# A fused three-mixer decoder layer on one core: the attention values of two pairs of heads in one group, even heads first

## The chip, the core and the metric

The kernel runs on one core of a Trainium2 chip. The metric is the device time of one execution in microseconds (us); three runs of the kernel before have a median of 263.72 us.

## What is computed

One decoder layer on a sequence of 256 positions with 1024 channels. A projection of the input feeds three mixers (a gated spatial MLP, a convolution module, attention with 8 heads of 64), their gates and the gates of a merge; each mixer's result is projected to 1024 channels, the three are merged, projected once more, added to the input and normalised. The part that the change touches is the last product of the attention and its gate. With a sequence of 256 and a block of 256 the attention is plain causal attention:

```
p   = softmax(q k^T / 8 - slope * distance)      # per head, causal
att = p @ v                                      # per head: 256 x 64
y_c = att * silu(c_g)
```

## The kernel before, in words

Everything is in float32. The large matrix products split each operand into a high part (hi, the cast to the TensorE's rounded float32 format, made by ScalarE at L92) and a low part (lo, the difference, made by VectorE at L93) and add three products, or two with a double-width moving operand. `gemm_tok` (L206, matmuls at L96 to L98) makes tiles with positions on the partitions, `gemm_ch` (L222, matmuls at L229 and L230) tiles with channels on the partitions. PLAN (L43) lists the blocks of the projection in the order in which they are computed: among them the query, key and value blocks, then the gate blocks `c_g` and `b_g`, then the first merge block `m0a`. Weights are loaded and split two to three half-blocks ahead (L596).

Between the blocks stand the small steps of the mixers. Which step is emitted behind which block is written out by hand in AFTER (L580): one list of steps for the middle of a block and one for its end. The framework then orders each engine's instructions itself: a step that was emitted later can be placed earlier, into a time at which the scheduler expects the engine to wait, and a step whose operands the scheduler expects late is placed later.

The steps of the attention, for each of the four pairs j of heads (2j is the even head, 2j + 1 the odd one; r is 0 or 1):

- `scores(j)` (L377) and `softmax(j)` (L391) leave the normalised probabilities in `lg[j]`: for each head 384 columns, 128 for the first 128 queries and 256 for the other 128 queries.
- `turn(j)` (L410) transposes the three 128 x 128 blocks of each head on TensorE (L415) and ScalarE copies them into a tile `turned` (L417). There are four buffers of `turned`, so two pairs of heads at a time.
- `values(j)` (L419) multiplies with the values (L426). Per head two matmuls: keys 0 to 127 for all 256 queries (256 columns, starts the sum) and keys 128 to 255 for the queries 128 to 255 (128 columns, adds to it). The stationary operand is 64 columns wide, the head's part of `v`; the output of an even head stands on partitions 0 to 63 of the accumulator `att`, that of an odd head on partitions 64 to 127, so that an even head uses the left half of TensorE's columns and an odd head the right half. The order of the four matmuls of a pair is even 256, odd 256, even 128, odd 128. Two pairs share one accumulator `att[j // 2]`, one of the four `aux` buffers in PSUM; after the second pair VectorE multiplies with the gate (L434) and the result is split into `yh[2]` and `yl[2]` (L435).

AFTER emits `turn(0)` and `turn(1)` at the end of block `c_g`; `values(0)`, `values(1)`, `turn(2)` and `turn(3)` in this order at the end of `b_g`; `values(2)` and `values(3)` in the middle of `m0a`.

## Time and profile before

| | before |
|---|---|
| median of 3 runs | 263.72 us (263.62 to 264.7) |
| the profiled execution's own time | 263.93 us |
| its span, first to last instruction | 262.2 us |
| TensorE (PE) busy | 253.0 us, 96% of the span |
| VectorE (DVE) busy | 214.1 us, 82% |
| ScalarE (ACT) busy | 151.2 us, 58% |
| matmuls of line 426 | 32 records for 16 instructions |

The profile shows one execution. The time outside of the span is 263.93 - 262.2 = 1.7 us. PE is TensorE's matmuls and PEld its loads of stationary operands, which run beside them. A matmul with plain float32 operands and a 64-column output appears as two records, two passes over its columns. Matmuls are pipelined: the time between two starts tells what one costs, and the duration of a record is longer than that.

### The profile page before, as it was taken

The page shows a single profiled execution, that of the slowest core. Times are in us where ns is not written, and L with a number is a line of the kernel's source. Part 1 is how long each engine was busy: PE and PEld are TensorE (multiplying, and loading weights), DVE is VectorE, ACT ScalarE, POOL GpSimd, SP SyncE. Part 2 cuts the span into 40 slices and gives each one's busy share as a digit, 9 for nine tenths or more (in the row PEclk, how much of TensorE's full clock was granted, in tenths as well). Part 3 has the DMA queues.
Part 4 walks back from the last instruction along what each step waited for, and adds up shares of the span by engine and source line. Part 5 has one row for each costly group of instructions (what it writes and reads, how often), then busy time and mean ns, then how long its engine had stood idle before and what let it go on. Part 6 is the DMA issues. An engine that isn't in the chain of part 4 may idle for free.

```text
span 262.2 us, 3445 instructions
## 1 busy us (share of the span) xinstructions
PE 253.0 (96%) x1284; PEld 212.4 (81%) x1284; DVE 214.1 (82%) x324; ACT 151.2 (58%) x220; POOL 20.4 (8%) x29
## 2 busy tenths in 40 slices
PE   6999999999999999999999999999999999999990
PEld 4888888889888888888877888888888888888880
DVE  1899998798389999999998999994689564794644
ACT  4884887999994446376556342354433895191201
POOL 6003000000000000000000000005054000000202
PEclk9999999999999999999999999999999999999996
DMA  6999999534435445484444354465543592000112
GB/s 183 345 422 411 420 415 336 191 135 162 160 120 200 159 164 180 157 302 164 161 162 160 111 209 164 142 220 214 225 162 139 189 373 102 0 0 0 44 39 80
DMA packets 9952, 49.31 MB, mean 188 GB/s; under 512 B 1104, under 2 KB 2512, under 8 KB 5072
## 3 DMA queue, kind: packets, MB, share of 16 engines
q1 hardware_dynamic: 9360, 48.51, 50.0%
q10 hardware_dynamic: 576, 0.59, 0.8%
q8 instruction: 10, 0.16, 0.2%
q14 instruction: 6, 0.05, 0.0%
HBM read 48.04 MB, written 1.05 MB: 187 GB/s over the span
## 4 chain that ended last, share of the span: by engine, by line
PE 73%; issue 21%; POOL 2%; DMA 1%; ACT 0%; POOLq 0%; SPq 0%; DVE 0%
PE mm L229 17%; PE mm L96 14%; PE mm L97 14%; PE mm L98 14%; PE mm L230 9%; PE aux L426 1%; DMA raw<-in_wts_dram 1%; PE aux L415 1%; POOL br L198 1%; PE aux L385 1%; PE aux L383 1%; PE aux L253 1%; POOL res L539 0%; POOL vr L198 0%; PE aux L450 0%
## 5 line engine op out<-in xcount | busy, mean ns | idle before, releaser
L92 ACT CAST hi<-raw 128x2048 fp32r<-128x2048 f32 (+3 forms) x64 | 83.1, 1319 | 66.3 <-PE mm L98 33.8
L93 DVE TENSOR_TENSOR lo<-raw,hi 128x2048 fp32r<-128x2048 f32 (+3 forms) x64 | 98.6, 1553 | 21.4 <-ACT hi L92 21.1
L229 PE MATMUL mm<-xs,hi 128*128 128x512 f32 x192 | 68.3, 399 | 0.0
L96 PE MATMUL mm<-hi,xs 128*128 128x512 f32 (+1 forms) x162 | 62.7, 396 | 1.0 <-ACT hi L92 1.0
L97 PE MATMUL mm<-lo,xs 128*128 128x512 f32 (+1 forms) x162 | 63.5, 392 | 0.0
L98 PE MATMUL mm<-hi,xs 128*128 128x512 f32 (+1 forms) x162 | 63.3, 391 | 0.0
L230 PE MATMUL mm<-xs,lo 128*128 128x256 f32 x192 | 54.0, 281 | 0.0
L280 DVE SCALAR_TENSOR_TENSOR cv<-glu,ch,cv 128x256 f32<-128x256 f32 x120 | 50.2, 477 | 0.0
L229 PEld LDWEIGHTS mm<-xs,hi 128*128 128x128 f32 x192 | 36.1, 188 | 8.8 <-DVE cv L280 0.2
L96 PEld LDWEIGHTS mm<-hi,xs 128*128 128x128 f32 x162 | 30.8, 193 | 7.5 <-ACT hi L92 1.5
L97 PEld LDWEIGHTS mm<-lo,xs 128*128 128x128 f32 x162 | 31.0, 191 | 6.7 <-issue 0.6
L230 PEld LDWEIGHTS mm<-xs,lo 128*128 128x128 f32 x192 | 36.3, 189 | 0.1
L98 PEld LDWEIGHTS mm<-hi,xs 128*128 128x128 f32 x162 | 31.0, 191 | 6.2
L97 PE MATMUL mm<-lo,yh 128*128 128x512 f32 x48 | 18.9, 393 | 0.0
L98 PE MATMUL mm<-hi,yl 128*128 128x512 f32 x48 | 18.8, 391 | 0.0
L96 PE MATMUL mm<-hi,yh 128*128 128x512 f32 x48 | 18.7, 389 | 0.0
L96 PE MATMUL mm<-hi,mth 128*128 128x512 f32 (+1 forms) x40 | 14.0, 349 | 0.0
L97 PE MATMUL mm<-lo,mth 128*128 128x512 f32 (+1 forms) x40 | 13.9, 349 | 0.0
L98 PE MATMUL mm<-hi,mtl 128*128 128x512 f32 (+1 forms) x40 | 13.7, 347 | 0.0
L470 ACT ACTIVATE gate<-mm 128x512 f32<-128x512 f32 x12 | 6.9, 596 | 11.2 <-PE mm L98 10.9
L297 POOL TENSOR_TENSOR csa<-cv 128x512 f32<-128x512 f32 x1 | 1.3, 1287 | 149.3 <-DVE cv L280 149.3
L234 ACT COPY low<-mm 128x256 f32<-128x256 f32 x24 | 8.5, 364 | 4.1 <-PE mm L230 4.0
(112 smaller groups left out, 250.8 us busy)
## 6 DMA issues: line engine op xcount, KB each, us to landing
raw<-in_wts_dram SPq DMA_DIRECT2D x38, 1024.0 KB, 4.8
raw<-in_wts_dram SPq DMA_DIRECT2D x4, 512.0 KB, 7.4
raw<-in_wts_dram SPq DMA_DIRECT2D x7, 256.0 KB, 5.6
xres<-in_x_dram SPq DMA_DIRECT2D x2, 512.0 KB, 6.1
fvec<-in_rows_dram SPq DMA_DIRECT2D x2, 512.0 KB, 8.0
out_dram<-res SPq DMA_DIRECT2D x4, 208.0 KB, 2.0
xr<-in_xt_dram SPq DMA_DIRECT2D x2, 256.0 KB, 6.1
vec<-in_rows_dram SPq DMA_DIRECT2D x1, 512.0 KB, 10.2
```

Of the source, the lines that this page charges most:

```text
L92: nc.scalar.copy(hi, src)
L93: nc.vector.tensor_tensor(lo, src, hi.bitcast(F32), op=ALU.subtract)
L96: nc.tensor.matmul(o, s[0], m[0], start=start, stop=False)
L97: nc.tensor.matmul(o, s[0], m[1], start=False, stop=False)
L98: nc.tensor.matmul(o, s[1], m[0], start=False, stop=stop)
L198: nc.gpsimd.tensor_tensor(r, ve, nhalf[:, 0:n], op=ALU.pow)
L229: nc.tensor.matmul(pt, his[i][:, cols], xs[k // 2][:, k % 2], start=k == 0, stop=False)
L230: nc.tensor.matmul(pt[:, 0], los[i][:, cols], x_part(k, 0), start=False, stop=k == KD - 1)
L234: nc.scalar.copy(low, pt[:, 1])
L253: nc.tensor.matmul(pz[:, g], sg_raw[:, g], vn[:, t, P * g:P * (g + 1)], start=True, stop=True)
L280: nc.vector.scalar_tensor_tensor(cv[:, c], src, w, cv[:, c], op0=ALU.mult, op1=ALU.add)
L470: nc.scalar.activation(gates[n][:, t], pt, AF.Sigmoid)
```

## The change

`values` is called once for two pairs (h = 0, 1) in place of once for each pair. It emits both even heads first, each with its 256-column and its 128-column matmul, and then both odd heads. The gate's product and the split follow as before. The accumulator is a local tile. In AFTER the two calls of each place become one.

```diff
-    att, turned = {}, {}
+    turned = {}
...
-    def values(j):
-        if j % 2 == 0:
-            att[j // 2] = aux_ps.tile([P, 2, S], F32, name="aux")
-        for b, (keys, q) in enumerate(((0, slice(0, S)), (1, slice(P, S)))):
-            for r in range(2):
-                d = HD * (2 * j + r)
-                w = turned[j, r][:, 0:S] if b == 0 else turned[j, r][:, S:]
-                nc.tensor.matmul(att[j // 2][HD * r:HD * (r + 1), j % 2, q], v[:, keys, d:d + HD], w,
-                                 start=b == 0, stop=b == 1)
-        if j % 2 == 1:
-            h = j // 2
-            if h == 0:
-                new_y(2)
-            c = slice(2 * h, 2 * h + 2)
-            y = work.tile([P, 2, S], F32, name="y")
-            nc.vector.tensor_tensor(y, gate_c[:, c], att[h], op=ALU.mult)
-            split(yh[2][:, c], yl[2][:, c], y)
+    def values(h):
+
+        att = aux_ps.tile([P, 2, S], F32, name="aux")
+        for r in range(2):
+            for jj in range(2):
+                d = HD * (2 * (2 * h + jj) + r)
+                w = turned[2 * h + jj, r]
+                o = att[HD * r:HD * (r + 1), jj]
+                nc.tensor.matmul(o, v[:, 0, d:d + HD], w[:, 0:S], start=True, stop=False)
+                nc.tensor.matmul(o[:, P:], v[:, 1, d:d + HD], w[:, S:], start=False, stop=True)
+        if h == 0:
+            new_y(2)
+        c = slice(2 * h, 2 * h + 2)
+        y = work.tile([P, 2, S], F32, name="y")
+        nc.vector.tensor_tensor(y, gate_c[:, c], att, op=ALU.mult)
+        split(yh[2][:, c], yl[2][:, c], y)
...
-        "b_g": ([], [at(values, 0), at(values, 1), at(turn, 2), at(turn, 3)]),
-        "m0a": ([at(values, 2), at(values, 3)], []),
+        "b_g": ([], [at(values, 0), at(turn, 2), at(turn, 3)]),
+        "m0a": ([at(values, 1)], []),
```

## Rows read from the trace of the kernel before

**Rows 1.** The page: span, and each engine's busy time, share, instructions

```profile
span 262.2 us, 3445 instructions
PE 253.0 (96%) x1284; PEld 212.4 (81%) x1284; DVE 214.1 (82%) x324; ACT 151.2 (58%) x220; POOL 20.4 (8%) x29
```

**Rows 2.** Busy time by stretch (columns in the first row)

```profile
core 0: us, PE busy (x) PEld busy (x) DVE busy (x) ACT busy (x) POOL busy (x), PEclk, DMA share, GB/s
123.30:128.90 5.60, 5.60 (x42) 4.32 (x41) 5.60 (x11) 2.09 (x2) 0.00 (x0) 1.00 0.16 44
128.90:143.20 14.30, 14.30 (x73) 10.94 (x72) 13.38 (x24) 8.59 (x14) 0.00 (x0) 1.00 0.56 205
143.20:200.00 56.80, 56.80 (x254) 47.02 (x253) 48.43 (x66) 24.58 (x19) 10.23 (x5) 1.00 0.47 167
200.00:255.00 55.00, 55.00 (x275) 46.46 (x273) 35.74 (x46) 25.37 (x37) 1.73 (x3) 1.00 0.29 105
```

**Rows 3.** All matmuls of line 426

```profile
L426 PE MATMUL aux<-turned,v x32: 272/351/431, 123.4 to 142.6; 128*64 128x256 f32 x16, 128*64 128x128 f32 x16
```

**Rows 4.** PE's timeline around its first stretch of line 426 (start us, us, instruction)

```profile
122.82 0.28 PE L230 MATMUL mm<-xs,lo 128*128 128x256 f32 x1
122.94 0.39 PE L229 MATMUL mm<-xs,hi 128*128 128x512 f32 x1
123.17 0.28 PE L230 MATMUL mm<-xs,lo 128*128 128x256 f32 x1
123.38 0.87 PE L426 MATMUL aux<-turned,v 128*64 128x256 f32 x8
124.18 0.50 PE L229 MATMUL mm<-xs,hi 128*128 128x512 f32 x1
124.51 0.28 PE L230 MATMUL mm<-xs,lo 128*128 128x256 f32 x1
```

**Rows 5.** The same around the second stretch

```profile
126.98 0.28 PE L230 MATMUL mm<-xs,lo 128*128 128x256 f32 x1
127.19 0.87 PE L426 MATMUL aux<-turned,v 128*64 128x256 f32 x8
128.00 1.20 PE L415 MATMUL aux<-ident,lg 128*128 128x128 f32 x9
```

**Rows 6.** The same around the third stretch

```profile
134.74 0.49 PE L415 MATMUL aux<-ident,lg 128*128 128x128 f32 x3
135.16 1.29 PE L426 MATMUL aux<-turned,v 128*64 128x256 f32 x10
136.38 0.50 PE L97 MATMUL mm<-lo,xs 128*128 128x512 f32 x1
136.72 0.39 PE L98 MATMUL mm<-hi,xs 128*128 128x512 f32 x1
136.95 0.40 PE L96 MATMUL mm<-hi,xs 128*128 128x512 f32 x1
```

**Rows 7.** The same around the fourth stretch

```profile
141.73 0.39 PE L96 MATMUL mm<-hi,xs 128*128 128x512 f32 x1
142.05 0.86 PE L426 MATMUL aux<-turned,v 128*64 128x256 f32 x6
142.84 0.50 PE L97 MATMUL mm<-lo,xs 128*128 128x512 f32 x1
143.19 0.40 PE L98 MATMUL mm<-hi,xs 128*128 128x512 f32 x1
```

**Rows 8.** PE's timeline around eight transposes with 128-column outputs

```profile
118.23 0.40 PE L229 MATMUL mm<-xs,hi 128*128 128x512 f32 x1
118.47 1.04 PE L450 MATMUL aux<-ident,ya 128*128 128x128 f32 x8
119.26 0.36 PE L230 MATMUL mm<-xs,lo 128*128 128x256 f32 x1
119.46 0.40 PE L229 MATMUL mm<-xs,hi 128*128 128x512 f32 x1
```

**Rows 9.** Line 426 in flight at 123.70 and 123.85, then at 136.15 and 136.24 us

```profile
123.38 0.65 PE L426 MATMUL aux<-turned,v 128*64 128x256 f32 x4
123.64 0.50 PE L426 MATMUL aux<-turned,v 128*64 128x256 f32 x4
...
135.86 0.59 PE L426 MATMUL aux<-turned,v 128*64 128x256 f32 x2
136.07 0.38 PE L426 MATMUL aux<-turned,v 128*64 128x256 f32 x1
```

**Rows 10.** Line 426 by form to 142.10 and 142.25; in flight at 142.485, 142.49

```profile
L426 PE MATMUL aux<-turned,v x2: 323/376/430, 142.1 to 142.1; 128*64 128x256 f32 x1, 128*64 128x128 f32 x1
L426 PE MATMUL aux<-turned,v x3: 272/323/430, 142.1 to 142.2; 128*64 128x128 f32 x2, 128*64 128x256 f32 x1
142.22 0.48 PE L426 MATMUL aux<-turned,v 128*64 128x128 f32 x2
142.32 0.38 PE L426 MATMUL aux<-turned,v 128*64 128x256 f32 x1
```

**Rows 11.** ACT's copies of the turned heads, and DVE's two gate products (timelines)

```profile
116.48 0.52 ACT L417 COPY turned<-aux 128x384 f32<-128x384 f32 x1
129.77 1.24 ACT L417 COPY turned<-aux 128x384 f32<-128x384 f32 x3
137.04 0.47 ACT L417 COPY turned<-aux 128x384 f32<-128x384 f32 x1
...
129.19 0.67 DVE L434 TENSOR_TENSOR y<-gate_c,aux 128x512 f32<-128x512 f32 x1
142.95 0.69 DVE L434 TENSOR_TENSOR y<-gate_c,aux 128x512 f32<-128x512 f32 x1 [0.84 <-PE aux L426]
```

## The prediction

> **What bounds the kernel now.** I read the page's first lines first: TensorE is busy for 253.0 of 262.2 us [rows 1]. Then the busy time by stretch: from 123.3 us, where the changed matmuls begin, to 255 us, TensorE is busy in every microsecond at the full granted clock (1.00), while VectorE has room after 200 us and ScalarE throughout [rows 2]. So a microsecond that TensorE spends more or less between 123 and 143 us moves the end by about as much. Nothing in the change adds work to another engine or a DMA, so the question is what sixteen matmuls cost on TensorE and how they are placed.

> Next I looked at line 426 alone. Sixteen instructions are 32 records, 16 with 256 columns and 16 with 128 [rows 3], two passes each. They run in four stretches: two of 8 records, one of 10, one of 6 [rows 4 to 7].

> **What a stretch costs.** I measure from a neighbouring matmul before to one behind and take off what lies between these two normally.
> - First stretch: L230 at 123.17 to L230 at 124.51 is 1.34 us; the same step without it is 0.35 (122.82 to 123.17) [rows 4]. Cost 0.99 us.
> - Second: 126.98 to 128.00 is 1.02, normally 0.12 (123.17 against 122.94 is 0.23 for an L229, and 0.35 - 0.23 is left for an L230) [rows 4, 5]. Cost 0.90.
> - Third: L415 at 134.74 to L98 at 136.72 is 1.98; three transposes (0.11 each) and an L97 (0.23, as from L98 to L96) are 0.56 [rows 6]. Cost 1.42.
> - Fourth: L96 at 141.73 to L98 at 143.19 is 1.46, normally 0.46. Cost 1.00 [rows 6, 7].

> Together 4.3 us.

> The inside of a stretch tells more. In the first one, two 256-column records are in flight from 123.38 on, two more join from 123.64, and by 123.85 four are under way that began at 123.64 or later: records come in pairs, 0.22 us a pair [rows 9]. In the third, the last two records have no partner, and their starts are 0.21 us apart (135.86, 136.07) [rows 9]: they are the two passes of the even head of the fourth pair, whose odd head was turned only later. So a pair costs what a single pass costs: an even head on one half of the columns and an odd head on the other half run at the same time. A 256-column pass is 0.215 us, a 128-column pass half of that; two of each, a whole head, are **0.65 us**, and an odd head beside it is free. The first stretch has 0.65 us of this, which leaves 0.99 - 0.65 = **0.34 us** for going to 64-column outputs and back. The eight transposes with 128-column outputs show no such price: 118.23 to 119.46 is 1.23, less 0.35 is 0.88, that is 8 times 0.11 [rows 8].

> **What the change does to each stretch.** The number of matmuls, of columns, of weight loads and of products on VectorE is the same. What moves is the order. Before, neighbours are an even and an odd head. After, the first four matmuls are all even, the last four all odd.

> Where the stretches are cut is the scheduler's choice. The first stretch is placed in front of a matmul of `b_g`, ahead of where the source has it, and takes exactly four matmuls (256, 256, 128, 128 columns) before that matmul goes on; by then all four heads were turned (the fourth copy starts at 116.48 [rows 11]), so time, not data, ended it. In the new order the first four are 256, 128, 256, 128: the same columns after three and after four. I take the cut to stay there.
> - First stretch, four matmuls of even heads: nothing to run beside. 2 x 0.65 = 1.30 in place of 0.65. **+0.65 us.**
> - Second stretch, the four of the odd heads: the same, **+0.65 us**.
> - Third stretch: before, five matmuls, since the odd head of the fourth pair was not turned (its copy starts at 137.04 [rows 11]). The new order has six ahead of that head: both even heads and the odd head of the third pair. If the two halves of the columns take their work independently, the even half with 1.30 us sets the time, against 0.65 + 0.43 = 1.08 now: +0.22 us. If an odd head starts only when the even ones have all been started, it is 1.30 + 0.65 less one 128-column pass that can overlap, 1.84: +0.76 us.
> - Fourth stretch: before, the odd head's two matmuls with the even head's 128 columns beside; after, the odd head alone. 0.65 both times: **0**.

> The sum is **+1.5 us** with independent halves and **+2.1 us** with order kept. Which one? The fourth stretch shows that a half can run ahead: one 256-column and one 128-column record start together, and at 142.22 a second 128-column record has started while the second pass of the first 256-column matmul starts only at 142.32 [rows 10]. Both passes of the 128-column matmul thus overtook a pass that precedes them. That is a jump over one pass; the change asks for a jump over seven or eight. The nearest row shows independent halves, so I take +1.5 and keep +2.1 for the range. Below zero in the third stretch a reason excludes, as long as the cut stands: its even half grows.

> [...]

> The rest I cost at nothing. The gate product of the first two pairs starts at 129.19, and the second stretch ends about 128.0 now [rows 5, 11]; 1.3 us later it waits some 0.1 us, and behind it in VectorE's queue stands work for TensorE that is late by the same 1.3 us. The second product waits 0.84 us already [rows 11]; that wait moves along. The copies into `turned` at 129.77 need their buffers free, which is so when the second stretch is over, before and after; the transposes that feed them stand behind it on TensorE in both orders. If that cover were gone, each is bounded by a tenth or two. SP's queue and POOL's are not passed by anything that moves.

> The profiled execution took 263.93 us, 0.2 over the median of 263.72; added to the median, the forecast is **265.2 us**.

> **The rivals.**
> 1. *Order kept in the same cuts*: +2.1, 265.8 us. For it: the trace shows a jump over one pass only. Against: that jump [rows 10]. Chance 0.25. [...]
> 2. *Not slower: one stretch for each group of eight, halves independent.* The scheduler places a whole group where now two stretches are, and the odd half starts at once. Each group is then 1.30 + 0.34 = 1.64, two are 3.3 in place of 4.3: -1.0, **262.7 us**. It decides as soon as a visit holds both halves' four matmuls. For it: a visit's 0.34 us is real, and two would go. Against: the first cut was set by time, and the copy at 137.04 keeps the last head out of the third stretch. Chance 0.17.
> 3. *One stretch each, order kept*: 2 x 1.30 - 0.11 + 0.34 = 2.83 a group, +1.4, 265.1 us. Chance 0.06.
> 4. *It does not do what it says*: the scheduler mixes the halves again as it fills gaps, and the pairs remain: about 263.7 us. Against: in the third and fourth stretch it held back the even head's 128 columns, whose operand was there, behind the odd head's matmul, so it keeps the source's order within an accumulator. Chance 0.10.

> **How the numbers follow.** The forecast has the remaining 0.42. Half a percent, about what a measurement here can tell from no change, is 1.3 us: under 262.4 is faster, over 265.0 slower. The forecast lies just beyond, and 0.27 of its 0.42 is counted as slower; of rival 1 0.24, of rival 3 0.03: 0.54. Rival 2 lies inside, and 0.07 of it is counted as faster. The rest, 0.39, is no difference. The range is 262.9 to 266.1: it holds the forecast, rivals 1, 3 and 4 and the upper edge of rival 2.

> **What the profile would show.** Right: four stretches of line 426 with 8, 8, 12 and 4 records; in the first two all starts one behind the other, 0.21 and 0.11 us apart, and a cost of about 1.64 us each; then 1.64 and 1.0. The third tells forecast and rival 1 apart: 1.64 or 2.2. Wrong: 16 records in one stretch, or pairs of records from 123.4 us on.

## The result and the profile after

The changed kernel takes **265.49 us** (median of 6 runs, 264.96 to 266.18) against 263.92 us for the kernel before in the same runs: ratio 1.0052, 95% interval 1.0035 to 1.0069. The medians differ by 1.57 us. The ratio is an estimate of its own and not the quotient of the two medians (that is 1.0059); by it the changed kernel is slower by 1.4 us, between 0.9 and 1.8. The ratios further down are of the same kind, each against the kernel before in the same runs. The forecast was 265.2.

The profiled execution took 265.72 us. The first lines of its page:

```profile
span 264.0 us, 3446 instructions
PE 255.1 (97%) x1284; PEld 214.0 (81%) x1284; DVE 214.1 (81%) x324; ACT 151.3 (57%) x220; POOL 19.4 (7%) x29
```

Each engine has as many instructions as in [rows 1], TensorE is busy for 2 us more, and the span is 1.8 us longer. To see where, I take two matmuls that both kernels have: the first transposes of `turn_a`, ahead of all matmuls of `values`, and the first matmul of the first branch projection, behind them. TensorE's timeline of the kernel after, and then the second of the two in the kernel before (the first one is in [rows 8]):

```profile
118.94 1.04 PE L449 MATMUL aux<-ident,ya 128*128 128x128 f32 x8
155.47 0.39 PE L96 MATMUL mm<-hi,yh 128*128 128x512 f32 x1
256.65 0.28 PE L98 MATMUL mm<-hi,mtl 128*128 128x256 f32 x1
```

```profile
153.67 0.39 PE L96 MATMUL mm<-hi,yh 128*128 128x512 f32 x1
254.84 0.28 PE L98 MATMUL mm<-hi,mtl 128*128 128x256 f32 x1
```

Between the two it was 153.67 - 118.47 = 35.20 us, and it is 155.47 - 118.94 = 36.53: **+1.33 us**. From there to the last matmul it is 101.17 before and 101.18 after. The remaining 0.47 us of the span lie ahead of 118.94, where the two programs are the same; over all profiles of this study the start of `turn_a` varies between 118.24 and 119.22. So I read each kernel by this distance as well as by its time. It is one profile for each kernel, and it is good to about 0.2 us: without the cost of the changed matmuls themselves, measured as in the prediction, it is 30.89 us before, 30.88 after, and between 30.8 and 31.0 in the third, sixth and seventh experiments.

The four stretches of the changed matmuls, now lines 427 (256 columns) and 428 (128 columns), in TensorE's timeline of the kernel after:

```profile
123.29 0.28 PE L230 MATMUL mm<-xs,lo 128*128 128x256 f32 x1
123.64 0.28 PE L230 MATMUL mm<-xs,lo 128*128 128x256 f32 x1
123.85 0.65 PE L427 MATMUL aux<-turned,v 128*64 128x256 f32 x2
124.33 0.38 PE L428 MATMUL aux<-turned,v 128*64 128x128 f32 x2
124.55 0.59 PE L427 MATMUL aux<-turned,v 128*64 128x256 f32 x2
125.07 0.50 PE L229 MATMUL mm<-xs,hi 128*128 128x512 f32 x1
125.41 0.28 PE L230 MATMUL mm<-xs,lo 128*128 128x256 f32 x1
...
127.84 0.28 PE L230 MATMUL mm<-xs,lo 128*128 128x256 f32 x1
128.05 0.32 PE L428 MATMUL aux<-turned,v 128*64 128x128 f32 x1
128.05 0.43 PE L427 MATMUL aux<-turned,v 128*64 128x256 f32 x1
128.21 0.27 PE L428 MATMUL aux<-turned,v 128*64 128x128 f32 x1
128.32 0.38 PE L427 MATMUL aux<-turned,v 128*64 128x256 f32 x1
128.54 0.38 PE L428 MATMUL aux<-turned,v 128*64 128x128 f32 x2
128.75 0.59 PE L427 MATMUL aux<-turned,v 128*64 128x256 f32 x2
129.19 0.38 PE L428 MATMUL aux<-turned,v 128*64 128x128 f32 x2
129.50 1.20 PE L415 MATMUL aux<-ident,lg 128*128 128x128 f32 x9
...
136.70 0.49 PE L415 MATMUL aux<-ident,lg 128*128 128x128 f32 x3
137.12 0.65 PE L427 MATMUL aux<-turned,v 128*64 128x256 f32 x2
137.60 0.38 PE L428 MATMUL aux<-turned,v 128*64 128x128 f32 x2
137.82 0.65 PE L427 MATMUL aux<-turned,v 128*64 128x256 f32 x4
138.25 0.44 PE L428 MATMUL aux<-turned,v 128*64 128x128 f32 x4
138.95 0.40 PE L97 MATMUL mm<-lo,xs 128*128 128x512 f32 x1
...
143.53 0.39 PE L96 MATMUL mm<-hi,xs 128*128 128x512 f32 x1
143.85 0.65 PE L427 MATMUL aux<-turned,v 128*64 128x256 f32 x2
144.34 0.38 PE L428 MATMUL aux<-turned,v 128*64 128x128 f32 x2
144.99 0.40 PE L98 MATMUL mm<-hi,xs 128*128 128x512 f32 x1
```

In the first stretch the even heads' passes stand one behind the other, six starts from 123.85 on, where before there were eight in four pairs [rows 4, 9]. In the second, one even matmul of 128 columns that the first stretch left over runs beside the first odd head; the rest is alone. In the third, the first even head is alone until 137.82, then even and odd passes come in pairs: four records of 256 columns start from 137.82 on, and from 138.25 on, 0.43 us later, four of 128; 0.43 us is what two passes of 256 columns take alone (in the kernel before, two such starts are 0.21 us apart [rows 9]). The profile does not name the half of a record; which is which follows from the program's order and from the starts, since records of one half stand a whole pass apart in these timelines (0.21 us with 256 columns, 0.11 with 128). Measured like before, each against its neighbours:

| stretch | before | forecast | after | change |
|---|---|---|---|---|
| first: 123.64 to 125.41, less 0.35 | 0.99 | 1.64 | 1.42 | +0.43 |
| second: 127.84 to 129.50, less 0.12 | 0.90 | 1.55 | 1.54 | +0.64 |
| third: 136.70 to 138.95, less 0.56 | 1.42 | 1.64 | 1.69 | +0.27 |
| fourth: 143.53 to 144.99, less 0.46 | 1.00 | 1.00 | 1.00 | 0 |
| sum | 4.31 | 5.83 | 5.65 | **+1.34** |

That is the whole of the +1.33 us between the two marks. The four stretches have 6, 10, 12 and 4 records.

### The profile page after: what moved, and what is told of

Read it like the earlier page. It is cut to its first block, busy times and chain, and to the rows that moved or that the text cites. A ratio compares the mean times of both kernels' runs of the same rounds, so it can differ in the third digit from the quotient of the medians.

```text
span 264.0 us, 3446 instructions
## 1 busy us (share of the span) xinstructions
PE 255.1 (97%) x1284; PEld 214.0 (81%) x1284; DVE 214.1 (81%) x324; ACT 151.3 (57%) x220; POOL 19.4 (7%) x29
## 4 chain that ended last, share of the span: by engine, by line
PE 73%; issue 21%; POOL 2%; DMA 1%; ACT 0%; POOLq 0%; SPq 0%; DVE 0%
PE mm L229 17%; PE mm L96 14%; PE mm L97 14%; PE mm L98 14%; PE mm L230 9%; PE aux L427 1%; DMA raw<-in_wts_dram 1%; PE aux L415 1%; POOL br L198 1%; PE aux L385 1%; PE aux L383 1%; PE aux L253 1%; PE aux L428 1%; POOL res L538 0%; POOL vr L198 0%
## 5 line engine op out<-in xcount | busy, mean ns | idle before, releaser
L229 PE MATMUL mm<-xs,hi 128*128 128x512 f32 x192 | 68.2, 399 | 0.0
L96 PE MATMUL mm<-hi,xs 128*128 128x512 f32 (+1 forms) x162 | 63.0, 400 | 0.7 <-ACT hi L92 0.7
L97 PE MATMUL mm<-lo,xs 128*128 128x512 f32 (+1 forms) x162 | 63.7, 393 | 0.0
L98 PE MATMUL mm<-hi,xs 128*128 128x512 f32 (+1 forms) x162 | 63.5, 392 | 0.0
L230 PE MATMUL mm<-xs,lo 128*128 128x256 f32 x192 | 54.0, 281 | 0.0
L280 DVE SCALAR_TENSOR_TENSOR cv<-glu,ch,cv 128x256 f32<-128x256 f32 x120 | 50.9, 497 | 0.0
L229 PEld LDWEIGHTS mm<-xs,hi 128*128 128x128 f32 x192 | 36.1, 188 | 9.0 <-DVE cv L280 0.4
L96 PEld LDWEIGHTS mm<-hi,xs 128*128 128x128 f32 x162 | 30.8, 193 | 7.5 <-ACT hi L92 1.2
L230 PEld LDWEIGHTS mm<-xs,lo 128*128 128x128 f32 x192 | 36.3, 189 | 0.1
L97 PEld LDWEIGHTS mm<-lo,xs 128*128 128x128 f32 x162 | 31.2, 193 | 6.3 <-DVE lo L93 0.2
L98 PEld LDWEIGHTS mm<-hi,xs 128*128 128x128 f32 x162 | 31.2, 193 | 6.3
L97 PE MATMUL mm<-lo,yh 128*128 128x512 f32 x48 | 18.9, 393 | 0.0
L98 PE MATMUL mm<-hi,yl 128*128 128x512 f32 x48 | 18.8, 391 | 0.0
L96 PE MATMUL mm<-hi,yh 128*128 128x512 f32 x48 | 18.7, 389 | 0.0
L96 PE MATMUL mm<-hi,mth 128*128 128x512 f32 (+1 forms) x40 | 14.0, 349 | 0.0
L97 PE MATMUL mm<-lo,mth 128*128 128x512 f32 (+1 forms) x40 | 13.9, 349 | 0.0
L98 PE MATMUL mm<-hi,mtl 128*128 128x512 f32 (+1 forms) x40 | 13.7, 347 | 0.0
```

Of the source, the lines that this page charges most:

```text
L96: nc.tensor.matmul(o, s[0], m[0], start=start, stop=False)
L97: nc.tensor.matmul(o, s[0], m[1], start=False, stop=False)
L98: nc.tensor.matmul(o, s[1], m[0], start=False, stop=stop)
L229: nc.tensor.matmul(pt, his[i][:, cols], xs[k // 2][:, k % 2], start=k == 0, stop=False)
L230: nc.tensor.matmul(pt[:, 0], los[i][:, cols], x_part(k, 0), start=False, stop=k == KD - 1)
L280: nc.vector.scalar_tensor_tensor(cv[:, c], src, w, cv[:, c], op0=ALU.mult, op1=ALU.add)
```

## The experiments

Two questions were left. Is it the order of the matmuls that costs, or the new grouping? And how far behind an even head may an odd head stand and still run beside it? The third stretch gives a first answer to the second: by the starts from 137.82 us on, the odd half begins there with the even half's fifth pass, when three are still to start. The expectations call this the window theory.

**The old order in the new grouping.** The only edit is in the loop of `values`:

```diff
-        for r in range(2):
-            for jj in range(2):
+        for jj, b, r in [(jj, b, r) for jj in range(2) for b in range(2) for r in range(2)]:
                 d = HD * (2 * (2 * h + jj) + r)
-                w = turned[2 * h + jj, r]
-                o = att[HD * r:HD * (r + 1), jj]
-                nc.tensor.matmul(o, v[:, 0, d:d + HD], w[:, 0:S], start=True, stop=False)
-                nc.tensor.matmul(o[:, P:], v[:, 1, d:d + HD], w[:, S:], start=False, stop=True)
+                nc.tensor.matmul(att[HD * r:HD * (r + 1), jj, P * b:], v[:, b, d:d + HD],
+                    turned[2 * h + jj, r][:, S * b:S + P * b], start=b == 0, stop=b == 1)
```

> One call for two pairs as in the changed kernel, but the matmuls in the old order: even and odd head by turns. The order theory (an odd head is free only when it is issued close behind an even one): four stretches of line 424 that cost 4.3 us in sum, as before, and the time of the kernel before, ratio 0.999 to 1.001 (about 263.9 us). The grouping theory (the single call and its local accumulator cost the time): the time of the changed kernel, ratio about 1.005 (265.4 us).

264.01 us against 264.08 before, ratio 0.9998 (0.9987 to 1.0008). The stretches have 8, 8, 10 and 6 records again, and the distance between the marks is that of the kernel before, 153.85 - 118.65 = 35.20 us:

```profile
118.65 1.04 PE L446 MATMUL aux<-ident,ya 128*128 128x128 f32 x8
153.85 0.39 PE L96 MATMUL mm<-hi,yh 128*128 128x512 f32 x1
```

The grouping costs nothing that shows. The loss is the order, together with the cuts that the scheduler makes in it: with the old order they are the old ones again.

**Even heads first, but each group whole.** Each matmul is pinned behind the one traced before it on TensorE, so that the scheduler cannot place it earlier, and the second group is moved to the end of `m0a`, where all heads are turned (the lines of the old loop, which go as above, are left out):

```diff
...
+        for r, jj, b in [(r, jj, b) for r in range(2) for jj in range(2) for b in range(2)]:
                 d = HD * (2 * (2 * h + jj) + r)
+                tc.keep_in_program_order(nc.tensor.matmul(
+                    att[HD * r:HD * (r + 1), jj, P * b:], v[:, b, d:d + HD],
+                    turned[2 * h + jj, r][:, S * b:S + P * b], start=b == 0, stop=b == 1))
...
-        "m0a": ([at(values, 1)], []),
+        "m0a": ([], [at(values, 1)]),
```

> The changed kernel's order, each group of eight matmuls held together in one stretch (pinned behind the matmuls emitted before it; the second group at the end of m0a). Window theory, from the third stretch of the changed kernel, where the odd half starts with the even half's fifth pass: the odd half starts when at most three even passes are still to start, so a group is 0.65 + 1.30 + 0.34 = 2.29 us, two are 4.6 in place of 4.3: 264.2 us (ratio 1.001), odd passes from about 0.65 us into the stretch. Order kept but for one pass: 2.83 a group, 265.3 us (1.005). Independent halves: 1.64 a group, 262.9 us (0.996).

264.24 us, ratio 1.0003 (0.9992 to 1.0015). The distance is 154.25 - 118.84 = 35.41 us, +0.21 where the window theory has +0.3, order kept +1.4 and independent halves -1.0:

```profile
118.84 1.04 PE L446 MATMUL aux<-ident,ya 128*128 128x128 f32 x8
154.25 0.39 PE L96 MATMUL mm<-hi,yh 128*128 128x512 f32 x1
```

The interval leaves out the ratios of the other two theories as well (1.005 and 0.996). The matmuls of line 424 by form, in the first 0.67 us of the first group and in the first 0.71 us (the columns after the count are shortest, median and longest duration in ns, then first and last start):

```profile
L424 PE MATMUL aux<-turned,v x4: 272/326/430, 126.5 to 127.1; 128*64 128x256 f32 x2, 128*64 128x128 f32 x2
L424 PE MATMUL aux<-turned,v x6: 272/379/431, 126.5 to 127.2; 128*64 128x256 f32 x4, 128*64 128x128 f32 x2
```

Until 127.20 four records, the first even head; by 127.24 six: the fifth even pass and the first odd one have come together. The second group's records last as long as the first one's, 2.22 us from the first start to the last end in both. That fits four even passes alone, four beside odd ones and the last four odd ones alone again: from the first group's first start at 126.53 to the transpose at 128.68 it is 2.15 us, three times 0.65 and 0.20.

**Even and odd by turns, each group whole.** The pins and the place of the run before, with the loop of the first experiment.

> Even and odd head by turns, each group of eight matmuls in one stretch (pinned, the second group at the end of m0a). The price of 0.34 us for each visit to 64-column outputs is paid twice in place of four times, and all passes go in pairs: 1.30 + 0.34 = 1.64 a group, 3.3 in place of 4.3: 262.9 us (ratio 0.996). If the price belongs to something else than the visit (each first matmul of a pair, or a wait that moves along), it stays: 263.9 us (1.000).

263.02 us, ratio **0.9951** (0.9934 to 0.9967). The distance is 153.23 - 119.22 = 34.01 us, -1.19:

```profile
119.22 1.04 PE L446 MATMUL aux<-ident,ya 128*128 128x128 f32 x8
126.69 0.28 PE L230 MATMUL mm<-xs,lo 128*128 128x256 f32 x1
126.91 1.52 PE L424 MATMUL aux<-turned,v 128*64 128x256 f32 x16
128.36 1.20 PE L415 MATMUL aux<-ident,lg 128*128 128x128 f32 x9
153.23 0.39 PE L96 MATMUL mm<-hi,yh 128*128 128x512 f32 x1
```

A group of 16 records now costs 128.36 - 126.69 - 0.12 = 1.55 us where the two first stretches of the kernel before cost 0.99 + 0.90. The second group, from L98 at 140.45 to L97 at 142.55 and less 0.46, costs 1.64 where the other two cost 1.42 + 1.00. Together it is 3.19, forecast 3.3.

**Whole heads by turns.** As the run before, with the loop `[(jj, r, b) ...]`: even head, odd head, even head, odd head.

> As the run before, but whole heads by turns: even head (256, 128), odd head (256, 128), and so on. Window theory (up to three waiting passes of one half may be passed over): the odd head still starts at once, 1.64 a group, 262.9 us (ratio 0.996), as the run before. Only neighbours run together (one pass may be passed over): four heads one behind the other less three overlaps of 0.11, 2.27 + 0.34 = 2.6 a group, 264.8 us (1.003).

263.14 us, ratio 0.9957 (0.9943 to 0.9971). The distance is 152.62 - 118.48 = 34.14 us, -1.06. With a whole head of four passes in front of the odd one, two groups take 0.13 us more than by pairs. The first group costs 127.66 - 125.95 - 0.12 = 1.59 us, 0.04 more than by pairs, where a jump over a single pass was estimated to give 2.6.

```profile
118.48 1.04 PE L446 MATMUL aux<-ident,ya 128*128 128x128 f32 x8
125.95 0.28 PE L230 MATMUL mm<-xs,lo 128*128 128x256 f32 x1
126.16 1.57 PE L424 MATMUL aux<-turned,v 128*64 128x256 f32 x16
127.66 1.20 PE L415 MATMUL aux<-ident,lg 128*128 128x128 f32 x9
152.62 0.39 PE L96 MATMUL mm<-hi,yh 128*128 128x512 f32 x1
```

**Passes or columns?** As the second run, with each 256-column matmul cut in two, twelve passes of 128 columns to a group's half (the two matmuls that go are left out):

```diff
...
+                for b, n, m in ((0, 0, 0), (0, 1, 1), (1, 1, 2)):
+                    tc.keep_in_program_order(nc.tensor.matmul(
+                        o[:, P * n:P * (n + 1)], v[:, b, d:d + HD], w[:, P * m:P * (m + 1)],
+                        start=b == 0, stop=(n, m) != (1, 1)))
...
```

> As e2_even_one_stretch (even heads first, one stretch a group), with each 256-column matmul cut into two of 128 columns, so that an even half has twelve passes of 128 columns in place of eight. Does the jump count passes or columns? By count, the odd half starts with the even half's ninth pass, when three are still to start, 0.92 us after the stretch's first start, and a group costs 0.87 + 1.30 + 0.34 = 2.51 us: 264.65 us (ratio 1.002). By columns (512 still to start in e2_even_one_stretch), it starts with the eighth pass, 0.81 us in: 264.45 us. If it has to wait for the last even pass: 1.25 us in, 265.3 us.

264.65 us, ratio 1.0026 (1.0012 to 1.0040); the distance is 154.12 - 118.24 = 35.88 us, +0.68. That excludes waiting for the last even pass (265.3 us), but the time alone does not part the count from the columns (264.65 and 264.45 both lie in the interval); the starts do. The two marks, then line 428 by form, in the first 0.92 us and in the first 0.94 us of the first group:

```profile
118.24 1.04 PE L451 MATMUL aux<-ident,ya 128*128 128x128 f32 x8
154.12 0.39 PE L96 MATMUL mm<-hi,yh 128*128 128x512 f32 x1
...
L428 PE MATMUL aux<-turned,v x8: 272/273/323, 125.9 to 126.7; 128*64 128x128 f32 x8
L428 PE MATMUL aux<-turned,v x10: 272/273/324, 125.9 to 126.9; 128*64 128x128 f32 x10
```

Eight even passes alone, and the first odd one starts with the ninth. Three are left again, though they are 384 columns here and 512 there. So between these two runs the count of passes left is the same, three, and the columns left are not. What is counted was not shown: every one of the changed matmuls has two passes, and the profile has a load of the stationary operand for every pass (32 PEld records beside the 32 of line 424 in the second run). Three passes still to start are also one whole matmul passed over, beside the one whose first pass has just started. No run has these matmuls with another number of passes, which would part these.

**Four complete pairs in four visits.** `values` by pairs again, pinned, placed in the middle and at the end of `b_g`, at the end of `m0a` and in the middle of `m0b`.

> Even and odd head by turns, every pair complete but in a stretch of its own (four visits, pinned: the middle and the end of b_g, the end of m0a, the middle of m0b). It parts the price of a visit from the passes without a partner. Visit theory: four times 0.65 + 0.34 = 3.96 us, 0.68 more than the two stretches of e3_pairs_one_stretch and 0.4 less than the kernel before, whose third stretch has 0.43 us of passes without a partner: 263.65 us (ratio 0.9985). If a visit costs nothing: the time of e3_pairs_one_stretch, 263.0 us (0.995).

263.96 us, ratio 0.9989 (0.9976 to 1.0002). That excludes a visit that costs nothing (0.995), but by itself it cannot tell the visit theory (0.9985) from no change at all. The distance is 153.81 - 118.94 = 34.87 us: -0.33 against the kernel before (forecast -0.4; the stretches' own cost falls from 4.31 to 3.89), and 0.86 more than with two visits (forecast 0.68; the four stretches themselves cost 3.89, 0.70 more than the two, and the rest lies outside of them and is not explained):

```profile
118.94 1.04 PE L453 MATMUL aux<-ident,ya 128*128 128x128 f32 x8
153.81 0.39 PE L96 MATMUL mm<-hi,yh 128*128 128x512 f32 x1
```

Both parts of the gain of the third run are there: two visits fewer (3.89 - 3.19 = 0.70 us), and no passes without a partner (4.31 - 3.89 = 0.42).

**All four pairs in one visit.** The copies behind the transposes go into the probabilities' own tile, and all 16 matmuls stand at the end of `m0a`, pinned, with `values` by pairs as in the run before (that part is left out here):

```diff
-            turned[j, r] = work.tile([P, DIST], F32, name="turned", bufs=4)
+            turned[j, r] = lg[j][:, r]
...
+        "b_g": ([], [at(turn, 2), at(turn, 3)]),
+        "m0a": ([], [at(values, j) for j in range(4)]),
```

> All four pairs in one stretch at the end of m0a, even and odd head by turns; the turned probabilities are copied back over the probabilities, so that eight heads have room. Visit theory: four times 0.65 and one 0.34, 2.94 us in place of 4.3: 262.65 us (ratio 0.995), 0.34 less than e3_pairs_one_stretch. Rival: the gate products and splits of all four pairs now stand close together and late on VectorE and ScalarE, and hold up the weights' splits: over 263.0 us.

262.66 us, ratio **0.9945** (0.9926 to 0.9964), the fastest version; the distance is 152.80 - 119.09 = 33.71 us, -1.49 (forecast -1.4).

```profile
138.72 0.39 PE L98 MATMUL mm<-hi,xs 128*128 128x512 f32 x1
139.04 2.82 PE L428 MATMUL aux<-lg,v 128*64 128x256 f32 x32
141.79 0.50 PE L96 MATMUL mm<-hi,xs 128*128 128x512 f32 x1
142.12 0.40 PE L97 MATMUL mm<-lo,xs 128*128 128x512 f32 x1
...
152.80 0.39 PE L96 MATMUL mm<-hi,yh 128*128 128x512 f32 x1
```

Between L98 at 138.72 and L97 at 142.12 lie 3.40 us, 0.46 of them normal: 2.94 us for all 16 matmuls, 4 x 0.65 + 0.34. The late gate products hold nothing up: between 130 and 170 us TensorE's longest wait is 0.4 us, at the value matmuls themselves, and it is for nothing that the profile shows. The intervals of this run and of the third one overlap; that it is the faster of the two rests on the distance, 0.30 us shorter, and on the matmuls themselves, 2.94 us against 3.19.

## Why the prediction was right

*TensorE sets the end between 123 and 255 us.* Right: all of the +1.33 us between the marks reaches the last matmul, which follows the second mark by 101.17 us before and 101.18 after.

*An odd head beside an even one is free, and it is the order that loses it.* Right, and shown by the first experiment: the old order inside the new grouping takes the old time, to 0.01 us in the distance. In these runs it was free only while it stood close behind: from a first group's first start to the transposes it was 1.45 us with one even matmul in front of the odd one, 1.50 with a head, and 2.15 with two heads, a limit that the prediction did not have.

*The first stretch keeps four matmuls.* Wrong: it took three, 256, 128 and 256 columns, so the stretches have 6 and 10 records in place of 8 and 8. The fourth, an even one, went to the second stretch and ran there beside an odd head. That is 0.22 us less than forecast (1.42 for 1.64). The equal number of columns after three matmuls was no sure sign of where the scheduler cuts; why it cut there was not tried.

*Second stretch +0.65, fourth 0.* Measured +0.64 and 0. The prediction's closing figure of 1.64 us for each of the first two is not its own sum for the second, which is 0.90 + 0.65 = 1.55; measured were 1.54.

*Third stretch: +0.22 with independent halves, +0.76 with order kept.* Measured +0.27, near the first, but neither picture is right. In the third stretch and in the second experiment (127.20 to 127.24 us) the odd half started with the fifth of eight even passes, not at once and not after the last. In the third stretch the even half had eight passes and the odd half four, and an odd half that starts with the fifth even pass is just done in time. With eight odd passes behind eight even ones the difference shows: 35.41 us in the second experiment, where independent halves would have given about 34.2 (an estimate, 35.20 less rival 2's 1.0). The reason for +1.5 was therefore half luck: the nearest row showed a jump over one pass, and I stretched it to seven. With four odd passes in the third stretch, a short jump and independent halves come to the same; with eight they would not have.

*Order kept (rival 1).* The third stretch parts it from the forecast: measured 1.69 us, where rival 1 has 2.2. Odd passes started while three even passes that precede them had not: from 137.82 us in the third stretch of the changed kernel, between 127.20 and 127.24 us in the second experiment, and with the ninth even pass of twelve, between 0.92 and 0.94 us into the group, in the fifth. For the fourth experiment the cost says it, 1.59 us for the first group, where the heads one behind the other, overlapping by one pass, were estimated at 2.6.

*One stretch for a group (rival 2).* It did not happen by itself, but forced it gives with pairs what the rival had: -1.19 us between the marks, where the rival had -1.0. With the changed order it does not: +0.21. So its condition of independent halves was wrong too.

*The price of 0.34 us for a visit.* It was measured again where full-width products stand on both sides: the one visit of the last experiment costs 2.94 - 2.60 = 0.34 over its passes. In front of the transposes the same measure gives less, 0.90 - 0.65 = 0.25 in the kernel before and 1.55 - 1.30 = 0.25 with pairs, so the forecasts with 0.34 for every visit were a little high. [rows 4] show a pause on either side: 0.21 us from the last L230 to the first value matmul, normally 0.12, and 0.33 from L229 at 124.18 to L230, normally 0.23. They show the pause and not its reason.

The 1.34 us of the profile agree with the 1.4 us of the ratio; the 1.57 us between the medians lie within the interval too.

## What to carry to other kernels

In these runs, matmuls whose outputs fill one half of the columns each went two at a time (0.22 us for a pair of 256-column passes), but only when their partners stood close behind in the instruction stream: put the two halves by turns (-1.19 us between the marks), or at most a head's four passes apart (two matmuls, -1.06 us), and not all of one half first (+0.21). Each separate stretch of such matmuls among full-width ones cost 0.25 to 0.35 us over its passes in the kernel before, so gather them in one place and check there that no operand arrives late and splits the group. A scheduler that fills gaps can cut a group anywhere, so an order that is good only when the group stays whole should be pinned.
